# Mixing norm: sums of squares in the middle of the first query group, later low parts behind the additions of squares

## The chip, the cores and the metric

The kernel runs on one core of a Trainium2 chip. TensorE (PE) multiplies matrices out of SBUF into PSUM; VectorE (DVE), ScalarE (ACT) and GpSimd (POOL) work on the results; SyncE (SP) and POOL issue transfers. Every engine works through its own list of instructions in order and waits on semaphores where one needs another's result. The metric is the device time of one execution in microseconds (us). The engines' order is fixed when the program is built.

## The reference

Two layers of a hybrid encoder on 512 tokens of width 1024, all in float32. Each layer is

```python
x = x + 0.5 * swiglu(rms_norm(x, ffn1_norm[l]), ffn1_w_gate[l], ffn1_w_up[l], ffn1_w_down[l])
h = rms_norm(x, mix_norm[l])
p = h @ w_in[l]
attn = mla_group(p[..., :o_kv], p[..., o_kv:o_pe], p[..., o_pe:o_cv], ...)
conv = conv_group(p[..., o_cv:], conv_w[l], conv_b[l], conv_ln_g[l], conv_ln_b[l])
x = x + jnp.concatenate([attn, conv], axis=-1) @ w_out[l]
x = x + 0.5 * swiglu(rms_norm(x, ffn2_norm[l]), ffn2_w_gate[l], ffn2_w_up[l], ffn2_w_down[l])
x = rms_norm(x, post_norm[l])
```

`rms_norm` divides each token by the root of its mean square and multiplies by a gain. `mla_group` is attention with 8 heads over low-rank query and key/value latents, `conv_group` a gated depthwise convolution over 31 taps with a layer norm. The change concerns the norm `h`, called the mixing norm here, and the first products of `h @ w_in`.

## The kernel before

**Layout and products.** x is held transposed, as 8 tiles of 128 features by 512 tokens. Every float32 operand of a product is split into a high and a low part, and `mm3` (L209 to L213) makes three matmuls of one product: high by high (L210), high by low (L211), low by high (L212). A weight column block comes with `load_w` (L154): a transfer by SP into one of 3 raw buffers (L156), the high part by ACT (L158), the low part as a subtraction by VectorE (L165). High and low parts lie in rings of 4 slots each. `in_turn` keeps the casts of ACT in the order in which the program writes them, and the subtractions of VectorE likewise: `turns[V]` holds the last of them, and the next is issued behind it.

**A norm put off.** A norm's factor belongs to the token, and tokens are the free dimension of the transposed products, so the products use x times the gain alone (`split_scaled`, high part L223, low part L224), and the factor R is multiplied in afterwards. R is made beside the products: `Stats.add` squares each of the 8 tiles on ACT (L240, L243) and adds them up (L247), for the mixing norm all on VectorE and behind the last L224. `sums` lets PE add over features (8 small matmuls in the profile, L254), `token` turns that into mean plus epsilon on VectorE (vtok, L261) and into its power of −0.5 on POOL (rtok, L229). The second call of the norm, step "R", spreads the factor over partitions by four transposes (L270) and copies it (L276).

**Order.** The end of the first feed-forward is followed by the mixing stage. PE does the products of the first two conv column blocks (`groups` with `WHOLE`, 48 matmuls), then the sums of the norm, then the steps of `SEQ`: q0 (first query block, 24 matmuls), R, c1 (third and fourth conv blocks), q1, q2, the latent keys and so on. One matmul of a group is called a product from here on, so the query group has 24. The conv's gating, which needs R, stands right behind the spread; the conv's taps on VectorE (L1014) begin behind the gating and are worked off through attention. The weights are asked for in the order first and second conv block, first query block, third and fourth conv block, second and third query block, latent keys; raw buffers and slots come free as earlier weights are used up.

`tc.issue_after(ins)` orders the instructions of a block behind `ins` on the same engine without a wait across engines. All else is ordered at build time by a planner with a model of the times.

Of the kernel before, what the change touches and what calls it, by code (L numbers as in the profile page):

```python
# [12 lines left out]
ALU = mybir.AluOpType  # L13
# [6 lines left out]
KD = D // P  # L20
# [13 lines left out]
WC = 1024  # L34
# [27 lines left out]
WOG = 4  # L62
CHAIN = 400
WAKE = 10
KS = (0, 2, 4, 6, 1, 3, 5, 7)
WOP = 4
EVP = "DAD"
# [17 lines left out]
def encoder_kernel(ctx: ExitStack, tc: tile.TileContext, xT, consts, vecs, rgain, wgu1, wd1, wdq1,  # L85
# [11 lines left out]
    def nm(s):  # L97
        uid[0] += 1
        return f"{s}{uid[0]}"

    def slot(dt=FP, w=S):
        return ring.tile([P, w], dt, tag="r", name=nm("r"))

    def tmp(w=S, dt=FP):
        return tmps.tile([P, w], dt, tag="t", name=nm("t"))

    def bank():
        return psum.tile([P, S], FP, tag="ps", name=nm("ps"))
# [14 lines left out]
    V, A, G, T = nc.vector, nc.scalar, nc.gpsimd, nc.tensor  # L123
# [12 lines left out]
    awake = bank()  # L136
    for _ in range(WAKE):
        T.matmul(awake[:, 0:P], ones, ones, start=True, stop=True)
# [15 lines left out]
    def load_w(src, w, kind="", queue=None):  # L154
        raw = wpool.tile([P, WC], FP, tag="raw", name=nm("raw"), bufs=3)
        (queue or nc.sync).dma_start(out=raw[:, :w], in_=src)  # L156
        hi = part(0)
        order["cast"] = in_turn("h", lambda: A.copy(hi[:, :w], raw[:, :w]))  # L158
        lo = low()
        if kind == "sum":  # L160
            A.activation(lo[:, :w], raw[:, :w], AF.Copy, scale=-1.0)
            G.dma_start(out=lo[:, :w], in_=src, accum_op=ALU.add)
            return hi, lo
        e = G if kind in POOLW.split() else V
        in_turn(e, lambda: e.tensor_tensor(lo[:, :w], raw[:, :w], hi[:, :w].bitcast(FP), ALU.subtract))  # L165
        return hi, lo
# [4 lines left out]
    def part(j, moved=False):  # L171

        if was[j] and not moved:
            used[j] += 1
        was[j] = moved
        i = (j * WN + used[j] % WN) * WC + (WOFF[j] if moved else 0)
        used[j] += 1
        return weights[:, i:i + WC]

    turns = {}  # L180

    def in_turn(key, make):

        with tc.issue_after(turns[key]) if key in turns else nullcontext():
            turns[key] = make().ins
        return turns[key]

    def low(moved=False):
        return part(1, moved)
# [14 lines left out]
    order = {}  # L204

    def ordered(name):
        return order[name]

    def mm3(o, lh, ll, rh, rl, first, last, free=False):  # L209
        T.matmul(o, lh, rh, start=first, stop=False, skip_group_check=free)  # L210
        T.matmul(o, lh, rl, start=False, stop=False, skip_group_check=free)  # L211
        order["mm"] = T.matmul(o, ll, rh, start=False, stop=last, skip_group_check=free).ins  # L212
        return order["mm"]  # L213
# [17 lines left out]
    class Stats:  # L231
# [5 lines left out]
        def add(self, src, scale=1.0, last=False, eng=None, apart=False, into=None):  # L237
            if self.acc is None:
                self.acc = slot() if into is None else into
                A.activation(self.acc, src, AF.Square, scale=scale)  # L240
                return
            sq = tmp() if into is None else into
            A.activation(sq, src, AF.Square, scale=scale)  # L243
            if apart:
                self.tail = sq
                return
            (eng or (V if last else G)).tensor_tensor(self.acc, self.acc, sq, ALU.add)  # L247

        def sums(self, made=bank):
            ps = made()  # L250
# [28 lines left out]
    def group(o, w, rhs, ks, n, ts=slice(0, S)):  # L279

        for k in ks:
            c = slice(k * P, (k + 1) * P)
            order["product"] = mm3(o, w[0][:, c], w[1][:, c], rhs[k][0][:, ts], rhs[k][1][:, ts], k == 0, k == n - 1)

    def groups(srcs, rhs, parts):

        ws = [load_w(src, WC) for src in srcs]
        os = [bank() for _ in srcs]
        for a, b in parts:
            for o, w in zip(os, ws):  # L290
                group(o, w, rhs, range(a, b), KD)
        return os
# [13 lines left out]
    def ffn_body(fpool, l, gx, norm, wgu, wd, wdq, wdr, gain, done, w0, halved, chunks, whole):  # L306
# [27 lines left out]
        def plain(os, ws, ks):  # L334
            for gu, o in enumerate(os):
                for k in ks if o is not None else ():
                    w = ws[k % 2]
                    c = slice(gu * 512 + k // 2 * P, gu * 512 + (k // 2 + 1) * P)
                    mm3(o, w[0][:, c], w[1][:, c], gx[k][0], gx[k][1], k == 0, k == KD - 1)

        def plain_first(os, ws):

            for k in KS:
                for gu, o in enumerate(os):
                    w = ws[k % 2]
                    c = slice(gu * 512 + k // 2 * P, gu * 512 + (k // 2 + 1) * P)
                    mm3(o, w[0][:, c], w[1][:, c], gx[k][0], gx[k][1], k == KS[0], k == KS[-1])

# [10 lines left out]
        def after(name):  # L359
            return tc.issue_after(order[name]) if name in order else nullcontext()  # L360
# [133 lines left out]
        def down(act, quarters_of, done=None):  # L494
# [7 lines left out]
            for g in range(2):  # L502
# [18 lines left out]
                with after("u0"):  # L521
                    add(0, 0, px, 1)
                times(py, a12, "b21", True, 1)
                with after("u"):
                    add(0, 0, py, 1)
                with after("first") if g else nullcontext():
                    V.tensor_tensor(s3[:, :n], a11[:, :n], a21[:, :n], ALU.add)
                with after("first"):
                    V.tensor_tensor(a21[:, :n], a21[:, :n], a22[:, :n], ALU.add)
                    V.tensor_tensor(a11[:, :n], a11[:, :n], a21[:, :n], ALU.add)  # L530
                times(px, a11, "t2", False)
                order["second"] = add(1, 0, px, -1)
                with after("second" if g == 0 else "first"):
                    V.tensor_tensor(a12[:, :n], a12[:, :n], a11[:, :n], ALU.add)  # L534
# [29 lines left out]
        for p0, p1 in chunks:  # L564
# [4 lines left out]
            for p in range(p0, p1) if not short else ():  # L569
# [21 lines left out]
                elif p < CHUNKS[0][1]:  # L591
                    for r in range(2):
                        ws = [load_w(wgu[l, p, 2 * r + q], WC) for q in range(2)]
                        o = [bank(), bank()]
                        if w0 and not r:
                            with tc.issue_after(order["mm"]):
                                plain(o[:1], ws, KS[:KD // 4])
                            with tc.issue_after(order["mm"]):
                                R = norm()
                            with after("spread"):  # L600
                                plain(o[:1], ws, KS[KD // 4:])
                                plain([None] + o[1:], ws, range(KD))
# [70 lines left out]
    def mix(l, gx, norm, done):  # L673
        with tc.tile_pool(name="k", bufs=4) as kpool:
            mix_body(kpool, l, gx, norm, done)

    def mix_body(kpool, l, gx, norm, done):
        u, order = [], {}
        diag = kpool.tile([P, PT, Q], FP, tag="m", name=nm("m"), bufs=11)
        G.tensor_tensor(diag, cst[:, None, CI32:CI32 + Q].to_broadcast([P, PT, Q]),  # L680
                        vv(l, "cp")[:, :, None].to_broadcast([P, PT, Q]), ALU.mult)
# [49 lines left out]
        q = kpool.tile([P, NT, H, DQ], FP, tag="q", name=nm("q"), bufs=1)  # L731
# [3 lines left out]
        ssk = small.tile([P, NT, H], FP, tag="ssk", name=nm("ssk"))  # L735

        def latent_q(j):
            ps = bank()
            group(ps, load_w(wql[l, j], WC, "q"), gx, range(KD), KD)
            pq.append(ps)  # L740

        def latent_q_out():
# [99 lines left out]
        def up_kv(w, t, n=S):  # L842

            ts_ = slice(t * P, (t + 1) * P)
            ps = bank()
            for k in range(2):
                cs = slice(k * n, (k + 1) * n)
                mm3(ps, ckT[k][0][:, ts_], ckT[k][1][:, ts_], w[0][:, cs], w[1][:, cs], k == 0, k == 1)
            return ps
# [20 lines left out]


        first = groups([wcv[l, 0], wcv[l, 1]], gx, WHOLE)
        rm = norm()
        for step in SEQ.split():
            if step == "R":
                R = norm()
                glu(*first)
            elif step[0] == "c":
                conv_in(int(step[1]))
            else:  # L880
                {"q0": lambda: latent_q(0), "q1": lambda: latent_q(1), "q2": lambda: latent_q(2), "qo": latent_q_out, "k": latent_k,
                 "kt": turn_latent_k, "tt": token_terms, "uq": queries, "uk": keys}[step]()
# [99 lines left out]
        with tc.issue_after(order["turned"]):  # L982
            for t in range(NT):
                ps = up_kv(wv, t)
# [54 lines left out]
        with tc.high_priority(CHAIN):  # L1039
# [10 lines left out]
            sums = ordered("sums")  # L1050
# [98 lines left out]
    gx = []  # L1149
# [5 lines left out]
    def half_w(q, gu):  # L1155
# [3 lines left out]
        in_turn(V, lambda: V.tensor_tensor(lo, raw, hi.bitcast(FP), ALU.subtract))  # L1159
    for m in KS:  # L1160
        if m:
# [8 lines left out]
    w0 += [load_w(wgu1[0, 0, q], WC) for q in (2, 3)]  # L1170
    gx = [gx[KS.index(m)] for m in range(KD)]
    with tc.issue_after(order["cast"]):
# [30 lines left out]
    norm = Norm(st)  # L1203
    for l in range(L):
        nx, st1, done = follow(l, "gm", True)
        ffn(l, gx, norm, wgu1, wd1, wdq1, None, vv(l, "g1"), done, w0 if l == 0 else None, chunks=SHORT, whole=True)
        gx = nx
        nx, st2, done = follow(l, "g2")
        mix(l, gx, Norm(st1), done)
        gx = nx  # L1210
# [3 lines left out]
        if l + 1 < L:  # L1214
# [10 lines left out]
            gx = nx  # L1225
# [23 lines left out]
            norm = NormPost(st3)  # L1249
# [102 lines left out]
```

## Time and profile before

| | us |
|---|---|
| three timed runs | 1744.59, 1746.3, 1748.67 |
| their median | 1746.3 |
| the profiled execution | 1744.13 |
| its span, first to last instruction | 1741.8 |
| sums of the mixing norm begin, layer 0 and 1 | 345.36, 1210.07 |
| R is spread, layer 0 and 1 | 355.00, 1216.50 |
| mean granted TensorE clock | 0.997 |

Times in the trace count from the start of the span. A group of instructions is named by engine, line, operation and tiles; a number in brackets behind it is the time for which its engine was idle before it, with the instruction that ended the wait. The granted clock is the share of full speed that PE had. Matmuls overlap: each shows some 0.39 us here, but they start 0.23 us apart, so distances between starts are to be read and not durations.

### The profile page before, as it was taken

What the parts mean: (1) busy time and instruction counts of PE and PEld (TensorE: products, weight loads), DVE (VectorE), ACT (ScalarE), POOL (GpSimd) and SP (SyncE); (2) the same over time, 40 slices, a digit from 0 to 9 for tenths busy, and PEclk for the clock granted to TensorE, in tenths of its full rate; (3) what the DMA queues carried; (4) which work ended last, traced back from release to release, by engine and by line L of the source; (5) the groups of instructions that cost most, each with busy time, mean ns of one, the idle gap of its engine ahead of it and who ended that gap; (6) DMA issues with size and microseconds to landing.
All of it is one profiled execution on the core that took longest, in us unless ns stands there. A gap on an engine that the chain in (4) does not pass through costs nothing. (4 is left out here: it accounts for less than half of the span.)

```text
span 1741.8 us, 31616 instructions
## 1 busy us (share of the span) xinstructions
PE 1723.8 (99%) x12576; PEld 1581.1 (91%) x12576; DVE 1463.9 (84%) x2099; ACT 1100.5 (63%) x1711; POOL 383.0 (22%) x342
## 2 busy tenths in 40 slices
PE   9999999999999999999999999999999999999997
PEld 7899999888678899999888999998976788999997
DVE  7988889978964989897679989898989559888887
ACT  5575767557953476756645757575778535757664
POOL 2001000047823101010320010110676410011110
PEclk9999999999999999999999999999999999999999
DMA  5567575524303467675326575754260125675743
GB/s 185 147 153 192 137 201 130 139 69 123 81 25 97 121 161 178 157 172 139 119 66 174 133 199 132 202 132 133 83 157 26 53 87 142 158 189 139 199 109 100
DMA packets 72692, 232.62 MB, mean 134 GB/s; under 512 B 8672, under 2 KB 10848, under 8 KB 72544
## 3 DMA queue, kind: packets, MB, share of 16 engines
q1 hardware_dynamic: 51984, 163.48, 29.3%
q0 software_dynamic: 20416, 67.12, 21.4%
q8 instruction: 98, 1.61, 0.4%
q14 instruction: 50, 0.41, 0.1%
q10 hardware_dynamic: 144, 0.00, 0.0%
HBM read 226.38 MB, written 2.10 MB: 131 GB/s over the span
## 5 line engine op out<-in xcount | busy, mean ns | idle before, releaser
L211 PE MATMUL ps<-r,weights 128*128 128x256 f32 (+1 forms) x2644 | 814.0, 308 | 0.1
L210 PE MATMUL ps<-r,weights 128*128 128x256 f32 (+1 forms) x2644 | 808.7, 309 | 1.0 <-ACT weights L1158 0.3
L212 PE MATMUL ps<-r,weights 128*128 128x256 f32 (+1 forms) x2388 | 741.1, 312 | 1.8 <-DVE weights L299 1.5
L210 PEld LDWEIGHTS ps<-r,weights 128*128 128x128 f32 x2644 | 497.1, 188 | 32.0 <-ACT weights L158 1.6
L211 PEld LDWEIGHTS ps<-r,weights 128*128 128x128 f32 x2644 | 497.2, 188 | 28.8 <-DVE r L224 0.5
L212 PEld LDWEIGHTS ps<-r,weights 128*128 128x128 f32 x2388 | 448.9, 188 | 33.7 <-DVE weights L299 2.5
L210 PE MATMUL ps<-xj,weights 128*128 128x256 f32 x864 | 238.5, 276 | 0.0
L211 PE MATMUL ps<-xj,weights 128*128 128x256 f32 x864 | 238.5, 276 | 0.0
L297 ACT CAST weights<-fr 128x1024 fp32r<-128x1024 f32 (+2 forms) x178 | 170.9, 960 | 89.3 <-DVE fr L451 45.8
L158 ACT CAST weights<-raw 128x1024 fp32r<-128x1024 f32 (+4 forms) x124 | 112.2, 915 | 176.8 <-PE ps L211 102.1
L299 DVE TENSOR_TENSOR weights<-fr,weights 128x1024 fp32r<-128x1024 f32 (+2 forms) x178 | 198.0, 1113 | 30.7 <-ACT weights L297 30.7
L431 POOL DMA_DIRECT2D ls<-in_wgu x72 | 62.9, 873 | 581.1 <-ACT ls L430 533.2
L165 DVE TENSOR_TENSOR weights<-raw,weights 128x1024 fp32r<-128x1024 f32 (+4 forms) x108 | 117.8, 1101 | 76.0 <-ACT weights L158 75.5
L210 PEld LDWEIGHTS ps<-xj,weights 128*128 128x128 f32 x864 | 162.2, 188 | 0.0
L211 PEld LDWEIGHTS ps<-xj,weights 128*128 128x128 f32 x864 | 162.2, 188 | 0.0
L212 PE MATMUL ps<-xj,ls 128*128 128x256 f32 x576 | 159.0, 276 | 0.0
L299 DVE TENSOR_TENSOR weights<-raw,weights 128x1024 fp32r<-128x1024 f32 (+2 forms) x112 | 124.0, 1107 | 14.6 <-ACT weights L297 14.3
L297 ACT CAST weights<-raw 128x1024 fp32r<-128x1024 f32 (+2 forms) x112 | 106.9, 954 | 42.8 <-DVE raw L534 24.4
L1020 POOL TENSOR_TENSOR y<-y,pr 128x495 f32<-128x495 f32 (+29 forms) x90 | 119.4, 1329 | 50.9 <-ACT pr L1018 45.6
L430 ACT ACTIVATE ls<-fr 128x1024 fp32r<-128x1024 f32 (+2 forms) x62 | 60.8, 980 | 104.6 <-PE ps L212 62.7
L518 DVE SCALAR_TENSOR_TENSOR x<-ps,x 128x512 f32<-128x512 f32 x154 | 105.5, 685 | 5.5 <-PE ps L212 5.0
L212 PEld LDWEIGHTS ps<-xj,ls 128*128 128x128 f32 x576 | 108.1, 188 | 0.0
(259 smaller groups left out, 2996.8 us busy)
## 6 DMA issues: line engine op xcount, KB each, us to landing
fr<-in_wgu SPq DMA_DIRECT2D x112, 512.0 KB, 4.7
ls<-in_wgu POOLq DMA_DIRECT2D x72, 512.0 KB, 7.3
raw<-in_wgu SPq DMA_DIRECT2D x62, 512.0 KB, 5.2
fr<-in_wdq SPq DMA_DIRECT2D x60, 384.0 KB, 5.1
ls<-in_wdq POOLq DMA_DIRECT2D x40, 384.0 KB, 5.8
raw<-in_wd POOLq DMA_DIRECT2D x32, 256.0 KB, 3.0
raw<-in_wcv SPq DMA_DIRECT2D x16, 512.0 KB, 3.3
raw<-in_wout SPq DMA_DIRECT2D x16, 512.0 KB, 3.6
```

Of the source, the lines that this page charges most:

```text
L158: order["cast"] = in_turn("h", lambda: A.copy(hi[:, :w], raw[:, :w]))
L165: in_turn(e, lambda: e.tensor_tensor(lo[:, :w], raw[:, :w], hi[:, :w].bitcast(FP), ALU.subtract))
L210: T.matmul(o, lh, rh, start=first, stop=False, skip_group_check=free)
L211: T.matmul(o, lh, rl, start=False, stop=False, skip_group_check=free)
L212: order["mm"] = T.matmul(o, ll, rh, start=False, stop=last, skip_group_check=free).ins
L297: in_turn("h", lambda: A.copy(hi[:, :w], src[:, :w]))
L299: order["lo"] = in_turn(V, lambda: V.tensor_tensor(lo[:, :w], src[:, :w], hi[:, :w].bitcast(FP), ALU.subtract))
L430: A.activation(lo[:, :n], src[:, :n], AF.Copy, scale=-1.0)
L431: G.dma_start(out=lo[:, :n], in_=w, accum_op=ALU.add)
L518: return V.scalar_tensor_tensor(v, o.rearrange("p (m t) -> p m t", m=2), 0.5 * sign, v, ALU.mult, ALU.add).ins
L1020: order["conv"] = G.tensor_tensor(ys[c][:, s:], ys[c][:, s:], pr[:, s:], ALU.add).ins
```

## The change

The sums of squares of the mixing norm (and `token` behind them) are no longer called between the first two conv blocks and q0, but inside q0, after `QS` = 4 of its 8 steps, by `issue_after`; the other four steps are issued behind the sums. `Stats.add` keeps its last addition, and when q0's own weight has been loaded, `turns[V]` is set to that addition, so that the low parts of all later weights (from the third conv block on) are issued behind it on VectorE.

```diff
+QS = 4
...
-            (eng or (V if last else G)).tensor_tensor(self.acc, self.acc, sq, ALU.add)
+            self.last = (eng or (V if last else G)).tensor_tensor(self.acc, self.acc, sq, ALU.add).ins
...
-        u, order = [], {}
+        u, order, order_of = [], {}, ordered
...
         def latent_q(j):
+            nonlocal rm
             ps = bank()
-            group(ps, load_w(wql[l, j], WC, "q"), gx, range(KD), KD)
+            w = load_w(wql[l, j], WC, "q")
+            if not j:
+                turns[V] = summed
+                group(ps, w, gx, range(QS), KD)
+                with tc.issue_after(order_of("product")):
+                    rm = norm()
+            with tc.issue_after(order_of("sums")) if not j else nullcontext():
+                group(ps, w, gx, range(0 if j else QS, KD), KD)
             pq.append(ps)
...
         first = groups([wcv[l, 0], wcv[l, 1]], gx, WHOLE)
-        rm = norm()
+        rm, summed = None, norm.st.last
```

## The prediction

> **What bounds the kernel now.** I read the page's busy shares first. TensorE (PE) is occupied nearly all the time, VectorE (DVE) comes next.
>
> ```profile
> PE 1723.8 (99%) x12576; PEld 1581.1 (91%) x12576; DVE 1463.9 (84%) x2099; ACT 1100.5 (63%) x1711; POOL 383.0 (22%) x342
> ```
>
> So a microsecond in which PE does nothing is a microsecond of the kernel, unless a later stage waits for something else anyway. The waits of PE over the whole trace say where it does nothing for a named reason (columns: total us, times, longest):
>
> ```profile
> PE ps L254 <- DVE r L247: 5.3, 3, 2.5
> PE ps L212 <- DVE weights L299: 1.5, 2, 1.2
> ```
>
> The largest is the matmuls that add up the squares (L254) waiting for VectorE's addition of squares (L247). Two of the three are the mixing norms, which the timeline of PE shows next: layer 0 first, then layer 1 (columns: start us, duration us, engine, line, what; a bracket gives the idle time before it and what ended it).
>
> ```profile
> 342.52 0.39 PE L212 MATMUL ps<-r,weights 128*128 128x512 f32 x1
> 345.36 1.36 PE L254 MATMUL ps<-ones,r 128*128 128x1 f32 x8 [2.46 <-DVE r L247]
> 346.59 0.77 PE L210 MATMUL ps<-r,weights 128*128 128x512 f32 x1
> 352.71 0.41 PE L212 MATMUL ps<-r,weights 128*128 128x512 f32 x1
> 354.77 0.39 PE L212 MATMUL ps<-r,weights 128*128 128x512 f32 x1
> 355.00 0.60 PE L270 MATMUL ps<-cst,rtok 128*128 128x128 f32 x4
> ...
> 1207.23 0.39 PE L212 MATMUL ps<-r,weights 128*128 128x512 f32 x1
> 1210.07 1.02 PE L254 MATMUL ps<-ones,r 128*128 128x1 f32 x8 [2.45 <-DVE r L247]
> 1210.96 0.48 PE L210 MATMUL ps<-r,weights 128*128 128x512 f32 x1
> 1216.28 0.39 PE L212 MATMUL ps<-r,weights 128*128 128x512 f32 x1
> 1216.50 0.60 PE L270 MATMUL ps<-cst,rtok 128*128 128x128 f32 x4
> ```
>
> The reader is to see one pattern twice: the last product of the first conv columns (342.52, 1207.23), 2.46 and 2.45 us of nothing, eight small matmuls of the sums, the 24 products of the first query group, and the spread of R (L270). But layer 1 takes 6.43 us from the sums to the spread (1210.07 to 1216.50) and layer 0 takes 9.64 (345.36 to 355.00) for the same instructions. The table by windows tells why (columns: window, length, busy time with instruction count for PE, weight loads, DVE, ACT, POOL, then granted PE clock, DMA share, GB/s):
>
> ```profile
> 343.00:347.00 4.00, 1.64 (x9) 1.67 (x10) 3.17 (x5) 1.30 (x2) 0.00 (x0) 0.86 0.31 97
> 350.00:353.00 3.00, 3.00 (x9) 2.28 (x9) 0.00 (x0) 0.00 (x0) 0.00 (x0) 0.55 0.00 0
> 353.00:356.00 3.00, 3.00 (x17) 2.50 (x16) 0.00 (x0) 0.98 (x2) 0.00 (x0) 1.00 0.00 0
> 1207.00:1211.00 4.00, 1.55 (x12) 1.15 (x10) 3.15 (x4) 1.99 (x2) 0.00 (x0) 1.00 0.16 30
> 1211.00:1215.00 4.00, 4.00 (x19) 3.31 (x20) 0.65 (x5) 0.00 (x0) 1.03 (x1) 1.00 0.61 192
> ```
>
> In layer 0 the granted clock falls at the sums (a mean of 0.86 over 4 us is 1.1 us at half rate, so at 345.9) and is back at 352.7, 6.8 us later: the matmuls from 346.59 to 352.71 stand about 0.43 apart, afterwards 0.23. In layer 1 the same gap leaves the clock at 1.00. So the clock's fall costs 9.64 − 6.43 = 3.2 us in this execution, once.
>
> Why is the addition late? VectorE's and ScalarE's timelines of layer 0:
>
> ```profile
> 334.54 2.36 DVE L165 TENSOR_TENSOR weights<-raw,weights 128x1024 fp32r<-128x1024 f32 x2
> 336.82 1.41 DVE L224 SCALAR_TENSOR_TENSOR r<-x,vec,r 128x512 fp32r<-128x512 f32 x2
> 338.14 4.39 DVE L247 TENSOR_TENSOR r<-r,t 128x512 f32<-128x512 f32 x6
> 343.39 1.23 DVE L165 TENSOR_TENSOR weights<-raw,weights 128x1024 fp32r<-128x1024 f32 x1 [0.85 <-ACT weights L158]
> 344.53 0.69 DVE L247 TENSOR_TENSOR r<-r,t 128x512 f32<-128x512 f32 x1
> 345.13 1.22 DVE L165 TENSOR_TENSOR weights<-raw,weights 128x1024 fp32r<-128x1024 f32 x1
> 346.76 0.16 DVE L261 TENSOR_SCALAR vtok<-ps 128x4 f32<-128x4 f32 x1 [0.41 <-PE ps L254]
> ...
> 338.86 1.36 ACT L243 ACTIVATE t<-x 128x512 f32<-128x512 f32 x2 [1.64 <-DVE r L247]
> 342.31 1.99 ACT L158 CAST weights<-raw 128x1024 fp32r<-128x1024 f32 x2 [2.09 <-PE ps L211]
> 355.01 1.05 ACT L158 CAST weights<-raw 128x1024 fp32r<-128x1024 f32 x1 [10.71 <-issue]
> ```
>
> Six of seven additions end at 342.53. The seventh has had its square since 340.2, but in VectorE's order the low part of the fourth conv weight (L165, 343.39) stands before it, and that waits for the ACT cast at 342.31, which waits for PE to leave the slot of the first conv weight. So PE's own last products delay, over ACT and DVE, the addition that PE then waits for.
>
> **The change, part by part.** It moves the eight matmuls of the sums (and vtok and the pow behind them) from ahead of the first query group to the middle of it: 12 of its 24 products, sums, 12 products. And it hangs all low parts from the third conv weight on behind the last addition.
>
> *The gap.* With the weights ready (two low parts end at 336.9; in the hand-written order they are the first query weight and the third conv weight), PE goes from 342.52 + 0.23 straight into the query group, and 12 products at 0.227 bring the sums to 342.75 + 2.72 = 345.47. Even if the last addition still ended at 345.22, as now, PE would not wait. In fact it ends sooner: the wait for the cast no longer stands before it, and the third conv weight's low part no longer stands before the two L224. Bounds for the last addition: at earliest about 341.9 (two L224 from 336.1, seven additions at 0.61), at latest 345.2. The gap goes for either.
>
> *The sums in the stream of products.* The trace has them there, at the norm ahead of the second feed-forward:
>
> ```profile
> 549.99 0.39 PE L212 MATMUL ps<-r,weights 128*128 128x512 f32 x1
> 550.21 0.95 PE L254 MATMUL ps<-ones,r 128*128 128x1 f32 x8
> 551.02 0.49 PE L210 MATMUL ps<-r,weights 128*128 128x512 f32 x1
> 551.35 0.40 PE L211 MATMUL ps<-r,weights 128*128 128x512 f32 x1
> 551.58 0.40 PE L212 MATMUL ps<-r,weights 128*128 128x512 f32 x1
> ```
>
> From 549.99 to 551.35 are 1.36 us; without sums the three starts would be 2 × 0.227 = 0.45 apart, so they cost 0.91.
>
> *The sum.* From the start of the last conv product to the spread there will be 0.23 + 24 × 0.227 + 0.91 = 6.6 us. Layer 0 has 355.00 − 342.52 = 12.5 now, layer 1 has 1216.50 − 1207.23 = 9.3. That is 5.9 and 2.7, together **8.6 us**, of which some 3.2 are the clock.
>
> *What is late next.* After the sums come vtok (0.16), POOL's pow and the spread:
>
> ```profile
> 347.00 1.04 POOL L229 TENSOR_TENSOR rtok<-vtok,minus_half 128x4 f32<-128x4 f32 x1 [15.53 <-DVE vtok L261]
> ```
>
> From the end of the sums (346.72) to the end of pow (348.04) are 1.3 us. Then 2.72 us of products hide it, and the spread doesn't wait, with 1.4 us to spare; that cover was 8.3 us before.
>
> *The low parts moved back.* Three, at 1.15 each, now run between the last addition and some 346 to 349, where VectorE has little to do. The earliest that PE needs (third conv weight) is due after the spread, near 349.5. Their raw buffers come free later, so SP issues later:
>
> ```profile
> 335.80 1.46 SPq L156 DMA_DIRECT2D raw<-in_wql  x2
> 344.64 2.06 SPq L156 DMA_DIRECT2D raw<-in_wkl  x2
> raw<-in_wql SPq DMA_DIRECT2D x6, 512.0 KB, 3.3
> ```
>
> The second transfer of the first row (third query weight) waits for the third conv weight's raw buffer: 343 to 346.5 instead of 336.9. It lands 3.3 later, by 350. Its cast waits anyhow for the end of the first query group (355.01 now, 349 then), and its products come after those of two conv and one query weight, 72 × 0.227 = 16 us after the spread. The latent-key transfers queued behind it in SP wait for the fourth conv weight's buffer (344.6 now, the same then). Cost: nothing. If that cover failed, it would be a wait of 1 to 3 us.
>
> *What follows.* Whether the 8.6 us reach the end depends on attention, where VectorE is the busiest:
>
> ```profile
> 400.00:450.00 50.00, 49.50 (x274) 38.30 (x272) 43.26 (x86) 36.95 (x67) 40.71 (x30) 1.00 0.60 159
> 450.00:500.00 50.00, 49.88 (x394) 33.66 (x393) 45.54 (x89) 38.27 (x95) 25.77 (x21) 1.00 0.01 3
> ```
>
> DVE is busy 43.3 and 45.5 of 50 us there. But all that it does there begins with R (the gating and the conv taps need it), and nothing of it is pulled into the present idle time before R. So a stage bound by DVE begins earlier by the same amount as PE does. The order of later instructions is laid by a planner at compile time, and the change alters the times it plans with. No row prices that. DVE's idle time in those two windows is 6.7 + 4.5 = 11 us a layer, and a quarter of it, won or lost, is ±3 a layer: I take 0 and keep −3 to +6 for the range.
>
> **The clock, weighed.** The rows: idle gaps of 2.46 and 2.45 us with the same sums behind them, the clock down once and not down once. The Trainium skill, "TensorE: Matmul & The Clock Gate", Part 1: The HAM clock gate, says that the rate halves after at least one idle window of about 3.4 us, and that the windows run free of the program. Taken literally, neither gap is long enough and the 3.2 us would not hang on it; with the eight small matmuls counted as idle, which the page does not say, 342.9 to 346.6 would do and the phase would decide. Read the first way, the low clock is not the gap's and can stay.
>
> **The rivals.**
>
> *The clock falls all the same* in one layer, because it is the stretch of sums that draws it down, not the gap. Price 3.2 us. For it: 2.46 us left the clock alone in layer 1. Against it: at 550.21 such sums stand between products, and from 551.35 to 551.58 the step is 0.23 again. It would be 1735.5 + 3.2 = 1738.7, with the offset below 1739.7; chance 0.12.
>
> *A new plan gives the gain back in attention.* For it: the DVE rows above have room for 11 us of loss or gain; against it: all planned times shift alike. At 6 to 8 us lost over both layers it is 1741.5 to 1743.5, with the offset 1742.5 to 1744.5, mostly within 0.2% of now; chance 0.13.
>
> *The norm's chain is caught behind a later low part: slower.* VectorE works in order. If the low part of the third query weight stands ahead of vtok there, vtok waits for its cast, and the cast for the end of the first query group. Now that costs nothing, as vtok runs at 346.76. With T the start of that group's last product: cast at T + 0.24 (355.01 − 354.77) for 1.05, low part 1.22, vtok and pow with their handovers 1.3, spread at T + 3.8. PE idles 3.6 us, longer than the gap that lowered the clock in layer 0, so 6.8 us at half rate follow, 3.4 more: 7 a layer. Layer 0 loses 1.1, layer 1 loses 4.3: 1744.1 + 5.4 = 1749.5, with the offset 1750.5. It decides at that one place in VectorE's order. Against it: vtok can start once the sums end, some 3 us before that cast can. Chance 0.07.
>
> *It does nothing* would need the sums still at the head of the group; the order is written out in the code, so 0.02.
>
> **How the numbers follow.** The profiled execution took 1744.13 us, of which the span is 1741.8. Less 8.6 is 1735.5. The median of the three runs, 1746.3, stands 2.2 above that execution; the spread of 4 us in these runs is about what the clock's fall in none, one or two of the layers would make (3 us each), and those falls go with the gap. So I count half of the 2.2 as offset that stays, and predict **1736.5**. Chance of this 0.66. The range reaches from 1732 (a lucky plan) to 1743.5 (clock rival, and most of the lost plan); I leave out the slower rival and the tails. About 0.2%, 3.5 us, is what a measurement here can tell from no change: 1742.8 to 1749.8 counts as same. Faster: 0.66, 0.12 and a little of the plan rival, 0.79. Same: the rest of it and "does nothing", 0.13. Slower: 0.08.
>
> **What would show it.** Right: in both layers no wait of L254 on L247; the sums 12 products into the query group, about 2.7 us after the last conv product; seven L247 in one row ahead of the L165; the spread 6.6 us after the last conv product; clock 1.00 throughout. Wrong: an idle PE ahead of L270 (the norm's chain is late); a granted clock below 1 at the sums although no gap precedes them; or both stages shortened as said, while the time from R's spread to the norm of the second feed-forward (550.2 − 355.0 = 195.2 us in layer 0) has grown, which would be the plan.

## The result: 0.65% faster, the gap gone in both layers

| | before | changed |
|---|---|---|
| median, 6 runs each | 1745.76 us | 1734.32 us |
| lowest to highest | 1742.65 to 1748.67 | 1733.48 to 1735.28 |
| profiled execution / its span | 1744.13 / 1741.8 | 1734.91 / 1732.4 |

The ratio is 0.9935, with a 95% interval of 0.9923 to 0.9948. Not only the median moved: the runs of the changed kernel lie within 1.8 us of each other, those of before within 6.

Lines from L64 on stand further down in the changed kernel, most by one: L211 to L213 are its products, L255 its sums, L248 its additions, L166 its low parts, L271 its spread. First the waits of PE over the whole trace (total us, times, longest), to be set against the two rows shown of before:

```profile
PE ps L213 <- DVE weights L300: 1.5, 2, 1.2
...
PE ps L255 <- DVE r L248: 0.2, 1, 0.2
```

The 1.5 us of the feed-forward's weights are as they were; of the 5.3 us of the sums 0.2 are left, and those belong to another norm, at the start of the kernel. PE's timeline around the mixing norm, layer 0 and then layer 1:

```profile
344.93 0.39 PE L213 MATMUL ps<-r,weights 128*128 128x512 f32 x1
345.16 0.94 PE L255 MATMUL ps<-ones,r 128*128 128x1 f32 x8
345.97 0.49 PE L211 MATMUL ps<-r,weights 128*128 128x512 f32 x1
346.29 0.40 PE L212 MATMUL ps<-r,weights 128*128 128x512 f32 x1
...
348.83 0.60 PE L271 MATMUL ps<-cst,rtok 128*128 128x128 f32 x4
...
1203.94 0.95 PE L255 MATMUL ps<-ones,r 128*128 128x1 f32 x8
...
1207.61 0.60 PE L271 MATMUL ps<-cst,rtok 128*128 128x128 f32 x4
```

No row has a bracket: nothing is waited for. From 344.93 to 346.29 are 1.36 us, the same as at the norm that the prediction took as its model. The query group's 12 first products reach back 2.72 us from 345.16, so the last conv product starts at 342.21 and the spread comes 6.62 us later; in layer 1 likewise (1207.61 − 1200.99). Before these were 12.5 and 9.3 us. VectorE, ScalarE, POOL and SP in layer 0:

```profile
337.13 5.18 DVE L248 TENSOR_TENSOR r<-r,t 128x512 f32<-128x512 f32 x7
342.23 1.22 DVE L166 TENSOR_TENSOR weights<-raw,weights 128x1024 fp32r<-128x1024 f32 x1
343.76 2.36 DVE L166 TENSOR_TENSOR weights<-raw,weights 128x1024 fp32r<-128x1024 f32 x2 [0.31 <-ACT weights L159]
346.14 0.16 DVE L262 TENSOR_SCALAR vtok<-ps 128x4 f32<-128x4 f32 x1
...
348.85 1.05 ACT L159 CAST weights<-raw 128x1024 fp32r<-128x1024 f32 x1 [4.17 <-PE ps L212]
...
346.38 1.04 POOL L230 TENSOR_TENSOR rtok<-vtok,minus_half 128x4 f32<-128x4 f32 x1 [15.23 <-DVE vtok L262]
...
335.49 8.37 SPq L157 DMA_DIRECT2D raw<-in_wql  x2
```

Seven additions stand in one row and end at 342.31, three low parts behind them, then vtok. The pow ends at 347.42, 1.4 us ahead of the spread. SP's row now reaches to 343.9: the third query weight is asked for 6.6 us later than before, and nobody notices, for its cast (348.85) waits for PE's end of the query group. The windows (as in the prediction, granted clock third from the end) show the clock at full speed through both stages:

```profile
343.00:347.00 4.00, 4.00 (x24) 3.42 (x23) 3.24 (x6) 1.68 (x2) 0.62 (x1) 1.00 0.53 154
347.00:355.00 8.00, 8.00 (x39) 6.60 (x38) 3.94 (x6) 5.44 (x8) 0.42 (x1) 1.00 0.39 136
1201.00:1205.00 4.00, 4.00 (x23) 3.49 (x22) 3.68 (x5) 2.00 (x2) 0.00 (x0) 1.00 0.40 126
```

Where else did time go? PE's starts of the same instructions, in us from each span's start, tell stage by stage:

| | before | changed | shift |
|---|---|---|---|
| R spread, layer 0 | 355.0 | 348.8 | 6.2 |
| norm of the second feed-forward, layer 0 | 550.2 | 544.0 | 6.2 |
| last product of the first conv blocks, layer 1 | 1207.2 | 1201.0 | 6.2 |
| R spread, layer 1 | 1216.5 | 1207.6 | 8.9 |
| norm of the second feed-forward, layer 1 | 1411.7 | 1402.8 | 8.9 |
| end of the span | 1741.8 | 1732.4 | 9.4 |

(1201.0 is the start worked out above.) The whole gain arises in the two stretches that the change touches (0.3 us of the first 6.2 lie ahead of it, 0.5 behind the last norm), and attention hands it on to the tenth.

### The profile page after: what moved, and what is told of

Its sections match the earlier page's. It is cut to its first block, busy times and chain, and to the rows that moved or that the text cites. A ratio compares the mean times of both kernels' runs of the same rounds, so it can differ in the third digit from the quotient of the medians.

```text
span 1732.4 us, 31618 instructions
## 1 busy us (share of the span) xinstructions
PE 1722.1 (99%) x12576; PEld 1581.1 (91%) x12576; DVE 1464.6 (85%) x2099; ACT 1101.0 (64%) x1711; POOL 382.6 (22%) x342
## 5 line engine op out<-in xcount | busy, mean ns | idle before, releaser
L211 PE MATMUL ps<-r,weights 128*128 128x256 f32 (+1 forms) x2644 | 807.7, 309 | 0.6 <-ACT t L425 0.3
L213 PE MATMUL ps<-r,weights 128*128 128x256 f32 (+1 forms) x2388 | 739.6, 312 | 1.7 <-DVE weights L300 1.5
L211 PEld LDWEIGHTS ps<-r,weights 128*128 128x128 f32 x2644 | 496.7, 188 | 31.6 <-ACT weights L159 1.8
L213 PEld LDWEIGHTS ps<-r,weights 128*128 128x128 f32 x2388 | 448.2, 188 | 33.0 <-DVE weights L300 2.1
L211 PE MATMUL ps<-xj,weights 128*128 128x256 f32 x864 | 238.5, 276 | 0.0
L166 DVE TENSOR_TENSOR weights<-raw,weights 128x1024 fp32r<-128x1024 f32 (+4 forms) x108 | 117.9, 1102 | 67.1 <-ACT weights L159 66.6
L211 PEld LDWEIGHTS ps<-xj,weights 128*128 128x128 f32 x864 | 162.2, 188 | 0.0
L213 PE MATMUL ps<-xj,ls 128*128 128x256 f32 x576 | 159.0, 276 | 0.0
L213 PEld LDWEIGHTS ps<-xj,ls 128*128 128x128 f32 x576 | 108.1, 188 | 0.0
```

## The experiments

Two things were to be told apart. Theory: the gap comes from VectorE's order and the clock falls because of the gap. Rivals: the clock falls because of the sums, or the gain is a new plan of the later stages.

**The kernel before, unchanged (e0_before).** For the clock of many runs.

> The kernel before, unchanged, for the granted clock of every run. If the fall of the clock hangs on the gap ahead of the sums and comes by chance, the runs fall into groups by mean clock: about 0.999 (no layer falls), 0.997 (one), 0.995 (two), with times near 1741, 1744 and 1747, 3 us a fall. If the spread of the times has another cause, runs of equal clock differ by as much as runs of different clock.

Measured: 1743.5 us over 11 runs, 0.9996 (0.9987 to 1.0004) against its own reference runs. Its profile has the same 2.5 us gap in both layers, but other falls of the clock:

```profile
343.00:347.00 4.00, 1.55 (x10) 1.42 (x10) 3.01 (x4) 1.56 (x2) 0.00 (x0) 0.90 0.26 69
347.00:351.00 4.00, 4.00 (x13) 3.16 (x14) 0.54 (x4) 0.00 (x0) 1.04 (x1) 0.67 0.50 156
1206.00:1210.00 4.00, 1.56 (x11) 1.44 (x12) 3.39 (x6) 1.38 (x2) 0.26 (x1) 0.97 0.29 80
1210.00:1214.00 4.00, 4.00 (x13) 3.15 (x12) 0.16 (x1) 0.00 (x0) 0.78 (x1) 0.60 0.48 145
```

In each layer the lost share (0.10 and 0.33 of 4 us) makes 1.7 us, that is 3.4 us at half rate: two short falls here, where the profile of the prediction had one of 6.8. The kernel is the same, so where and how long the clock falls is chance. The expected three groups did not come out as such. Over the 43 runs of this kernel in this and the next group of experiments, 0.998 goes with a mean of 1742.0 us (6 runs), 0.997 with 1743.7 (20), 0.996 with 1744.7 (10), 0.995 with 1745.5 (4) and 0.994 with 1745.8 (3): time goes with the clock, but runs of clock 0.997 alone reach from 1741.2 to 1745.5. Part of the spread has another cause, which stays open.

**Half the change: low parts only (e1_lows_only, again d2_lows_only).** The sums stay ahead of the query group.

```diff
         def latent_q(j):
...
             if not j:
                 turns[V] = summed
-                group(ps, w, gx, range(QS), KD)
-                with tc.issue_after(order_of("product")):
-                    rm = norm()
             with tc.issue_after(order_of("sums")) if not j else nullcontext():
-                group(ps, w, gx, range(0 if j else QS, KD), KD)
+                group(ps, w, gx, range(KD), KD)
...
-        rm, summed = None, norm.st.last
+        with tc.issue_after(order_of("product")):
+            rm = norm()
+        summed = norm.st.last
```

> Only the low parts behind the additions; the sums stay ahead of the query group. If the gap came from VectorE's order, the last addition ends near 342.3 in layer 0, before the last conv product, the gap shrinks to 0.3 us or less, the clock stays, and the time is that of the changed kernel, 1734 to 1735. If the place of the sums in the query group is what brings the gain, the time stays near 1740 to 1745.

Measured: 1735.43 us, ratio 0.9952 (0.9938 to 0.9965). PE and VectorE in layer 0:

```profile
342.58 0.39 PE L213 MATMUL ps<-r,weights 128*128 128x512 f32 x1
342.84 1.02 PE L255 MATMUL ps<-ones,r 128*128 128x1 f32 x8
...
337.51 5.19 DVE L248 TENSOR_TENSOR r<-r,t 128x512 f32<-128x512 f32 x7
```

The additions end at 342.70, and the sums start 0.26 after the last conv product, with no gap at all. So moving the sums isn't needed.

**The other half: sums only (e2_sums_only, again d3_sums_only).**

```diff
             if not j:
-                turns[V] = summed
                 group(ps, w, gx, range(QS), KD)
```

> Only the sums moved into the query group; the low parts are not ordered behind the additions. By the prediction's bounds (last addition at 345.2 at the latest, sums due at 345.5) the gap goes as well, the clock stays, 1734 to 1735. If both parts are needed, a wait of the sums on L248 stays in the trace and the time is 1736 or more.

Measured: 1735.63 us, ratio 0.9955 (0.9942 to 0.9967); no wait of the sums. VectorE in layer 0:

```profile
334.72 2.36 DVE L166 TENSOR_TENSOR weights<-raw,weights 128x1024 fp32r<-128x1024 f32 x2
337.00 1.41 DVE L225 SCALAR_TENSOR_TENSOR r<-x,vec,r 128x512 fp32r<-128x512 f32 x2
338.33 5.18 DVE L248 TENSOR_TENSOR r<-r,t 128x512 f32<-128x512 f32 x7
344.93 2.36 DVE L166 TENSOR_TENSOR weights<-raw,weights 128x1024 fp32r<-128x1024 f32 x2 [1.42 <-PE ps L212]
```

The third conv weight's low part stands ahead of the last L225 again, as before. But the planner, with the sums due later, now puts all seven additions ahead of the fourth conv weight's low part by itself. They end at 343.51, and the sums come at 345.65. This half, too, removes the gap alone.

Both halves had come out a microsecond over the changed kernel, on another chip, so they ran again beside it (d1_after is the changed kernel):

> The changed kernel, on the same chip as the two half changes beside it: 1734.2.

> Only the low parts behind the additions, again, beside the changed kernel. Either half alone removes the gap: within 1 us of it. If the sums' place adds something of its own, 1 us or more slower, as 1735.43 against 1734.18 on another chip hinted.

> Only the sums moved, again, beside the changed kernel. Either half alone removes the gap: within 1 us of it. If the order of the low parts adds something of its own, 1 us or more slower, as 1735.63 against 1734.18 on another chip hinted.

Measured: 1734.49 (ratio 0.9939, 0.9924 to 0.9953), 1734.21 (0.9939, 0.9925 to 0.9952) and 1735.51 us (0.9945, 0.9931 to 0.9959). The low parts alone give the whole gain. The sums alone are 1 us behind in the medians with overlapping intervals; whether that is real stays open.

**The cover of the norm's chain taken away (e3_qs7).** The sums after 7 of 8 steps.

```diff
-QS = 4
+QS = 7
```

> The sums after 7 of 8 steps instead of 4: 3 products (0.68 us) cover vtok and pow instead of 12. From the start of the sums to the end of pow the changed kernel takes 2.3 us, and 0.81 + 0.68 + some 0.1 cover 1.6 of it, so PE should stand idle some 0.8 us ahead of the spread in each layer: 1.6 us slower than the changed kernel, near 1736. If the norm's chain doesn't count, 1734.3.

Measured: 1736.4 us, ratio 0.9959 (0.9946 to 0.9971). The waits of PE, in layer 0 and layer 1:

```profile
PE ps L271 <- POOL rtok L230: 0.6, 1, 0.6
...
PE ps L271 <- POOL rtok L230: 0.5, 1, 0.5
```

The wait stands where it was expected, ahead of the spread, at 0.6 and 0.5 us instead of 0.8. The 1.1 us are the part of the 1.9 us over the changed kernel (1734.49 on another chip) that the trace shows; the rest is within what these runs scatter.

**The changed kernel again, as a control (c0_after).**

> The changed kernel again, as the control of this group on the same chip. With nothing left of the gap no run's clock falls inside the span except at its end, and the runs lie within 2 us of each other, near 1734.5. If the sums alone drew the clock down, falls would show here.

Measured: 1734.18 us (1733.57 to 1734.87), against 1744.15 for the kernel before on the same chip, ratio 0.9947 (0.9935 to 0.9959). In both profiles of the changed kernel, this one and that of the result, the clock stays at full speed from the start-up to the last ten microseconds, past all the sums that stand between products. So the sums alone don't draw it down.

**The gap made longer (g1_gap_more).** The kernel before with two more VectorE instructions ahead of the sums; the result is unchanged by them.

```diff
         first = groups([wcv[l, 0], wcv[l, 1]], gx, WHOLE)
+        for _ in range(2):
+            V.tensor_scalar(norm.st.acc, norm.st.acc, 1.0, None, ALU.mult)
         rm = norm()
```

> The kernel before with two multiplications by 1.0 of the finished sum of squares on VectorE, ahead of the sums: they stand behind another low part, so the gap grows from 2.46 to some 4.4 us in each layer. If the clock's fall hangs on the length of the stretch without products, it now falls in both layers in every run; gap 2 x 2 us plus two falls of 1.7 to 3.4 us against the one or two falls of before: 1749 to 1752. If the falls have nothing to do with the gap, only the 4 us are added: 1748.

Measured: 1749.49 us (1748.28 to 1752.61), ratio 1.0036 (1.0025 to 1.0048), at the lower end of what was expected. PE's wait, of the same length in both layers, the sums of layer 0, and the windows of layer 0 and then layer 1:

```profile
PE ps L254 <- DVE r L874: 4.4, 1, 4.4
...
347.33 1.84 PE L254 MATMUL ps<-ones,r 128*128 128x1 f32 x8 [4.39 <-DVE r L874]
...
345.00:347.00 2.00, 0.00 (x0) 0.00 (x0) 1.97 (x4) 0.00 (x0) 0.00 (x0) 0.60 0.65 185
346.00:353.00 7.00, 5.67 (x19) 4.88 (x20) 1.75 (x7) 0.00 (x0) 1.04 (x1) 0.56 0.37 115
...
1208.00:1212.00 4.00, 0.00 (x0) 0.00 (x0) 3.67 (x5) 1.21 (x2) 0.00 (x0) 1.00 0.32 100
1213.00:1220.00 7.00, 7.00 (x21) 5.70 (x21) 0.59 (x4) 0.00 (x0) 1.04 (x1) 0.56 0.15 56
```

Now both layers spend nearly all of the 7 us shown at half rate (0.56). The first window settles what the clock needs: from 345 to 347 PE does nothing at all, and the clock, at 0.60 over these 2 us, falls at 345.4. That is some 2.4 us after the end of the last conv product (342.95) and 1.9 us ahead of the first of the sums, so the gap alone lowers it. In layer 1 the clock still stands at 1.00 through 4 us without work and falls only at 1212.3, when the sums have just begun, so the moment of the fall varies.

What a fall costs depends on where it lies: in layer 0 some 2 us of it pass inside the gap, where a slow clock costs nothing. From the start of the last conv product to the spread are 13.5 us in layer 0 and 14.4 in layer 1. Two of the six runs have a mean clock of 0.996 and the others 0.994, so falls as long as these in every run are not shown.

**A gap elsewhere, without sums (g3_pow_late, g4_pow_later).** The changed kernel with multiplications by 1.0 on POOL between vtok and pow, three or four of them; the result is unchanged.

```diff
-            rsqrt(r, self.ve)
+            ve = self.ve
+            if slow:
+                late = tmp().rearrange("p (t c) -> p t c", t=NT)
+                ve = ve[:, :, None].to_broadcast([P, NT, P])
+                for _ in range(slow):
+                    G.tensor_tensor(late, ve, ones[:, None, :].to_broadcast([P, NT, P]), ALU.mult)
+                    ve = late
+                ve = late[:, :, 0]
+            rsqrt(r, ve)
...
-                    rm = norm()
+                    rm = norm.r = norm.st.token(D, slow=3)
```

> The changed kernel with three multiplications by 1.0 on POOL (some 1.3 us each, 128x512) between vtok and pow: PE should stand idle ahead of the spread some 2.5 us in each layer, a gap as long as that of before but with no sums in it. Gap alone: 2 x 2.5 = 5 us, 1739.5. If a gap of 2.5 us without the sums behind it is too short, the clock stays; if the gap's 2.5 us are enough, runs fall in part of the layers and the times spread as those of before, 1740 to 1745.

> The same with four multiplications: idle ahead of the spread some 3.8 us in each layer, the gap that the slower rival of the prediction was priced with (3.6 idle and 3.4 for the clock, 7 a layer). By that price 1734.5 + 14 = 1748 to 1749. If a gap of this length leaves the clock alone, 1742; if the clock falls for one 3.4 us stretch and not two, 1745.5.

Measured: 1747.19 us with three (ratio 1.002, 1.0011 to 1.0028) and 1750.42 with four (1.0036, 1.0023 to 1.005). Both are slower than expected, in part because the gaps were longer than meant: with three multiplications the pow behind them took 1.91 us, with four it took 1.04, but the last three multiplications took 1.6 each. PE's waits in layer 0, three and then four multiplications:

```profile
PE ps L279 <- POOL rtok L230: 3.2, 1, 3.2
PE ps L729 <- DMA r<-m: 1.3, 1, 1.3
```

```profile
PE ps L279 <- POOL rtok L230: 4.5, 1, 4.5
PE ps L729 <- DMA r<-m: 2.2, 1, 2.2
```

And the windows behind the gap of each layer, of the kernel with three and of the one with four:

```profile
353.00:357.00 4.00, 4.00 (x14) 3.21 (x12) 2.41 (x4) 3.57 (x5) 0.00 (x0) 0.57 0.17 63
...
1219.00:1223.00 4.00, 3.73 (x13) 3.04 (x14) 2.11 (x4) 3.01 (x5) 0.22 (x1) 0.68 0.27 74
```

```profile
354.00:358.00 4.00, 3.79 (x13) 3.24 (x14) 2.11 (x4) 2.61 (x4) 0.15 (x1) 0.63 0.03 10
...
1224.00:1228.00 4.00, 3.67 (x12) 3.10 (x13) 2.07 (x4) 2.49 (x4) 0.28 (x1) 0.58 0.06 22
```

With four, layer 0 has one more fall, behind the 2.2 us wait for the transfer, which ends at 449.21:

```profile
448.00:453.00 5.00, 3.79 (x24) 0.90 (x25) 1.83 (x3) 2.50 (x7) 3.81 (x4) 0.66 0.66 257
```

The clock falls in both layers with no sum in the gap; after 3.2 us of nothing a stretch of about 3.4 us at half rate costs 1.7. A gap also cost more than itself: with three, 6.4 of gaps, 3.4 of clock and the 1.3 us of a later wait for a transfer make 11.1 of the 13.0 us over the control. The remaining 1.9 were not followed; the planner gave the later stages another order here.

## Why the prediction was right, and where it was off

*The gap* went in both layers, for the reason given. That either half of the change is enough is what e1_lows_only and e2_sums_only show. The early bound of the last addition was a little too early: it counted 0.61 us an addition, and the seven took 0.74 each (5.18 us), so that the last ended at 342.31 and not at 341.9.

*The sums in the stream* cost 1.36 us from start to start, as read off the other norm; *the stretch* came out at 6.62 us against 6.6. The working against the profiled execution gave 1735.5 us, and the profiled execution of the changed kernel took 1734.91.

*The cover* of vtok and pow had 1.4 us to spare, as computed, and e3_qs7 shows the wait that appears without it.

*The low parts moved back* and the late transfer cost nothing: no wait for them appears.

*What follows* passed the gain on whole: 195.2 us from R's spread to the next norm before and after, and likewise in layer 1. The rival of a new plan was wrong here, though g3_pow_late shows that a plan can turn out otherwise.

*The clock* was rightly laid to the gap, and the rival that the sums draw it down fell: sums without a gap leave it alone (both profiles of the changed kernel), a gap without sums lowers it (g3_pow_late), and in layer 0 of g1_gap_more it falls before the first of the sums has run. The Trainium skill, "TensorE: Matmul & The Clock Gate", Part 1: The HAM clock gate, has windows of 3.4 us that run free of the program. The stretches at half rate of 3.4 and 6.8 us agree with that, as does their chance place in two profiles of one kernel. Its idle window of about 3.4 us does not agree if taken literally: gaps of 2.5 us with sums behind them, and of 3.2 without, were enough, and in g1_gap_more the fall came some 2.4 us after the last product's end.

*The step that failed* is the offset. The prediction added half of the 2.2 us by which the median of before stood above its profiled execution, "as offset that stays". None stayed: the median of the changed kernel stands 0.6 us below its profiled execution. That the prediction came out 2.2 us high is mostly this term; the remaining 0.6 is the step from the working's 1735.5 to the profiled 1734.91. The reason given beside it, that the spread comes from falls that go with the gap, is not shown to explain the 2.2 us either. Over 43 runs the mean clock of before (given to 0.001 a run) is short of full speed by 6.1 us of span, that of 11 runs of the changed kernel by 2.7. These 3.4 us went, but the profiled execution of before had lost as much to its one fall (6.8 us at half rate), so the 8.6 us of the working already held them. The 43 runs, on two chips, have medians of 1743.5, 1744.27 and 1744.15, so there before shows hardly any offset from its profiled 1744.13; on the chip of d1_after its median is near 1746 again. So the gain is 10.0 us on the chip of c0_after and 11.4 in the result; what makes before slower in the one than in the other stays open.

*The price of the slower rival* was 7 us a layer with 3.6 us of idle PE. g4_pow_later has 4.5 and costs (1750.42 − 1734.18) / 2 = 8.1 a layer. The total is near, but its parts are not: the clock's share was 3.4 us a layer in the working, and behind the spread the profile with four lost some 1.7 in each layer (0.37 and 0.42 of 4 us in the windows shown, and a little ahead of them). The rest is the longer gap and, in layer 0, the later wait for a transfer of 2.2 us with a fall of its own behind it, 1.7 more (0.34 of 5 us). Gaps, clock and this wait add up to 16.4 us; the medians differ by 16.2, but the two profiled executions (1752.58 and 1733.57) by 19.0, so some 3 us of that profile are not followed. That this order of VectorE occurs was not tried.

## What to carry to other kernels

When the busiest engine waits, look at what stands ahead of the late instruction in its own engine's order: here one weight preparation that wasn't urgent, itself waiting on the busiest engine, and reordering it was enough. Moving the consumer into the middle of other work cures the same wait from the other side, as long as enough work is left behind it to cover what follows (12 products did, 3 did not). Where a gap also lowers the clock, as gaps of 2.2 to 4.6 us did in some layers or all here, closing it is worth more than its length; the runs came out closer together as well, for reasons that the clock explains only in part.

## What was not expected of the hardware

The same gap in the same kernel cost one fall of 6.8 us at half rate in one profile and two falls of 3.4 in another: 3.4 us lost both times, in different layers. And the pow on POOL is not one size. Its group in the kernel before (min, median and max in ns):

```profile
L229 POOL TENSOR_TENSOR rtok<-vtok,minus_half x8: 1033/1042/1972, 27.1 to 1412.9; 128x4 f32<-128x4 f32 x8
```

The same 128x4 operation takes 1.04 us in the mixing norms and up to 1.97 in others; behind the three multiplications of g3_pow_late it took 1.91, behind the four of g4_pow_later 1.04. The cover of the norm's chain, 1.4 us here, would have been 0.5 with the longer one. What makes it long was not tried.
